# Two groups of values ahead of the recurrence instead of four, and the rest beside its steps

## Chip, cores and metric

The kernel runs on one core of a Trainium2 chip. The metric is the device time of one execution in microseconds (us); lower is better. Engines are called as the profile does: PE (TensorE matmul), PEld (its weight loads), DVE (VectorE), ACT (ScalarE), POOL (GpSimd), SP (SyncE, which issues nearly all DMAs).

## What is computed

A trunk of two layers over 256 tokens of 2048 channels: a pooling mixer and a gated feed-forward block (5632 wide), then an RWKV-7 time mixer and another feed-forward block, and a last norm. The change touches the RWKV-7 mixer alone. Cut to what matters:

```python
xr, xw, xk, xv, xa, xg = (h + xx * mu[j] for j in range(6))   # xx: h shifted by one token, minus h
r, k, v = xr @ w_r, xk @ w_k, xv @ w_v                        # 2048 x 2048 each
w_log, a, g = ...                                             # narrow (LoRA) projections
def step(state, inp):                                         # 32 heads of 64, 256 tokens
    r_t, w_t, k_t, v_t, a_t, b_t = inp
    sa = einsum('bhvk,bhk->bhv', state, a_t)
    state = state * w_t + sa[..., None] * b_t + v_t[..., None] * k_t
    return state, einsum('bhvk,bhk->bhv', state, r_t)
# y: group norm per head, plus a bonus (r k r_k) v, times g, then @ w_o
```

## The kernel before

Matmuls of weights are done in a split form: a weight or an activation is held as a high and a low part of type float32r, and three matmuls (high x high, high x low, low x high) are summed. `split_weights` (L149 to L151) loads a [128, 1024] tile of weights by DMA from SP's queue, makes the high part by a copy on ACT and the low part by a subtraction on DVE. The residual stream `h` is token-major in SBUF.

The recurrence is run in four chunks of 64 tokens, with the heads in 16 pairs, and the pairs in eight groups of two. Per group there are these parts, each written as a Python generator that yields after each *piece*:

- `values(gi)`, 4 pieces: token-major values of a group. A piece is one split tile of weights and 24 matmuls of 128 x 256 (L398 to L400), into one bank of PSUM (`acc`, three banks, shared with the output projection). After the fourth, ACT copies the bank to a tile `vt` (L403). The 16 tiles `xv` that all values read are made by the mix `mu_v`.
- `prepare(gi)`, 7 pieces: decay and rates (L435 to L440), a running sum (L448), decayed keys and receptances KB and AR, which go to DRAM (`dKB`, L474, L475), the triangular matrices M (L485, L487, to `dM`, L489), and the bonus.
- `invert(half)`, 18 pieces, one for each half of the groups: reads M back (L506), does 31 rows of two DVE instructions, each on the result of the one before (L515, L516), stores the result to `dZ` (L519), and a transposed copy (L520) to `dW` (L521). It has no matmul.
- `ready(gi)`, 6 pieces: loads KB and AR back (L714, L715), transposes (L722), makes masked products G of them (L733, L735), loads the inverse's blocks (L745, L748, L750), and joins them with two rounds of small matmuls (L756, L763, copies at L758 and L765).
- `chains(gi)`, 12 pieces: the recurrence proper, three pieces a chunk (L788 and L791; L797, the first that needs the inverse; L802 and L806 with the state's update on DVE).
- `head_norm(gi)` with the gate (L839 to L841), and `out_proj` (L903 to L905), which adds two groups' share of the output projection, 512 columns a piece pair.

`weave(main, others)` issues `main` piece by piece and spreads the pieces of each other generator evenly from a first to a last piece of main. What it writes is an order of priority. A planner (the scheduler of the framework) then goes through all instructions with a timeline of its own: on each engine it takes the first in priority that can run, so later work fills holes; a tile is given when a buffer of its tag is free. The order so found is fixed for each engine's queue.

A group's chains begin `STAG` = 8 steps after those of the group before, so there are 68 steps. Ahead of and beside them, before the change:

- **Stage A**, dense: values of groups 0 to 3 (16 pieces), the gate's narrow projection with its mixes (17 pieces over the first 12), `invert(0)` (18 pieces over the first 14).
- **Stage B**: `LV` = 6 pieces of values of group 4 on; 14 pieces of preparation of groups 4 to 7; `ready(0)`.
- **Stage C**, the 68 steps. Beside them: `ready(1)` to `ready(7)`; the other 10 pieces of values up to step `VL` = 20; the other 14 pieces of preparation up to step `PE_` = 8; `invert(1)` from step 8 to `IE` = 16; normalisation of each group from 12 to 18 steps after its start; the output projection, in parts, from step 26 on.

Preparation of groups 0 to 3 is done earlier, beside the receptances. Values of groups 0 to 3 lie in tiles of the pool `mx`, those of the others in four tiles (`vt`, `bufs=4`) of a pool that opens after stage A. `mx` has `MX` = 40 slots of [128, 512] and holds besides: the mixes `xv`, keys and receptances of the later pairs, KB, AR and their transposes, y, squares, gates, normalised ys, the last projection's weights, and G of groups 4 and 5 (G of groups 0 and 1 lies in `h`, that of others in eight tiles of their own).

Of the kernel before, what the change touches and what calls it, by code (L numbers as in the profile page):

```python
# [29 lines left out]
MX = 40  # L30
# [5 lines left out]
HP, VL, HNL = 30, 20, 6  # L36
LV, LP, PE_, IE = 6, 14, 8, 16
# [7 lines left out]
# columns of the [128, .] table of shape-only constants  # L45
# [3 lines left out]
def _consts():  # L49
    parts = []  # L50

    def put(name, a):
        a = np.ascontiguousarray(a, dtype=np.float32).reshape(128, -1)
        at = sum(p.shape[1] for p in parts)
        _COLS[name] = (at, at + a.shape[1])
        parts.append(a)

    p = np.arange(128)
    put("ident", np.eye(128))
    # pooling over tokens: rows are source tokens of a half, columns target tokens  # L60
    t = np.arange(T)
    p0 = np.zeros((128, 4, 144))
    p1 = np.zeros((128, 4, 128))
    for g, w in enumerate(WINDOWS):
        cnt = np.minimum(t + 1, w)
        band = ((t[None, :] >= t[:, None]) & (t[None, :] < t[:, None] + w)) / cnt[None, :] - np.eye(T)
        p0[:, g] = band[:128, :144]
        p1[:, g] = band[128:, 128:]
    put("pool0", p0)
    put("pool1", p1)  # L70
    # gram masks: rows (k | b) or (b | k), columns (r | a) or (a | r); b carries the factor -1/2
    j = (p % 64)[:, None]
    c = np.arange(64)[None, :]
    incl, strict = (j <= c).astype(np.float32), (j < c).astype(np.float32)
    even_rows = np.where(p < 64, 1.0, -0.5)[:, None]
    odd_rows = np.where(p < 64, -0.5, 1.0)[:, None]
    put("gmask", np.concatenate([incl * even_rows, strict * even_rows, strict * odd_rows, incl * odd_rows], 1))
    put("mmask", strict * -0.5)
    put("scan", np.tile((t % 64 != 0).astype(np.float32)[None], (128, 1)))
    put("twice", p[:, None] % 32 == np.arange(32)[None])  # L80
    put("heads", np.stack([p < 64, p >= 64], 1))
    put("rowscale", np.concatenate([even_rows, odd_rows], 1))
    return np.ascontiguousarray(np.concatenate(parts, 1))
# [7 lines left out]
def hybrid_encoder(ctx: ExitStack, tc: tile.TileContext, I, out):  # L91
# [5 lines left out]
    # residual stream, token-major: h[i][n] is [128 tokens, 512 channels]  # L97
# [28 lines left out]
    def load_sqrt(after):  # L126
        """have the table of Sqrt loaded by the time that its argument is there"""
        nc.scalar.activation(warm, after, AF.Sqrt, bias=epsr[:, 0:1], scale=0.0)
# [3 lines left out]
    # ---------------------------------------------------------------- helpers  # L132
    last = {}       # instructions that others are queued behind
# [4 lines left out]
    def split_weights(src, step=1024, tiles=None):  # L138
        """DRAM [P, n] -> list of (hi, lo) float32r tiles of step columns"""
# [15 lines left out]
    def split_act(dst, src, P=128):  # L155
        """fp32 [P, 256] -> float32r [P, hi 256 | lo 256]"""
        nc.scalar.copy(dst[:P, :256], src)
        nc.vector.tensor_sub(dst[:P, 256:], src, dst[:P, :256].bitcast(F32))
# [17 lines left out]
    def newton(r, v):  # L176
        """one step of r -> r (1.5 - 0.5 v r r); v is overwritten"""
# [4 lines left out]
    # ---------------------------------------------------------------- pooling  # L182
    def pool_layer():
        with tc.tile_pool(name="plc", bufs=1) as pl, tc.tile_pool(name="plp", bufs=1, space=PSUM) as ps:
# [18 lines left out]
            def pooled(g):  # L203
                """weights of a group, its pooled channels"""
# [42 lines left out]
    # ---------------------------------------------------------------- ffn  # L247
    def ffn(layer, each=None):
        gcol = par[f"g2_{layer}"]
        with ExitStack() as st:  # L250
            fg = st.enter_context(tc.tile_pool(name="ffg", bufs=1))     # written last, so in the place of what is read last before
# [62 lines left out]
    # ---------------------------------------------------------------- rwkv  # L314
    def weave(main, *others):
        """issue main piece by piece; others: (generator, its pieces, first and last piece of main to spread them over)"""
# [12 lines left out]
    def chained(*gens):  # L329
        for gen in gens:  # L330
            yield from gen

    def rwkv():
        with ExitStack() as st:
# [12 lines left out]
            # derived per-channel parameters  # L347
# [16 lines left out]
            rn = lp.tile([64, 256], F32R, name="rn")      # per head: hi, and lo below  # L364
            ends = misc[:, 820:884].rearrange("p (a b) -> p a b", b=4)
            bonus = misc[:, 884:948].rearrange("p (a b) -> p a b", b=32)
            kh = (slice(0, 64), slice(64, 128))     # token rows of k in an even and an odd chunk; b has the others

            # scratch: (k | b) and (r | a) of each pair, and the triangular systems of each half of the pairs
# [17 lines left out]
            def values(gi):  # L387
                """token-major values of two head pairs"""
                acc = acc_bank()
                av = acc.rearrange("p (i c) -> p i c", i=2)  # L390
                for u in range(4):
# [9 lines left out]
                    if u == 3:  # L401
                        vts[gi] = mx(F32, "vt") if gi < 4 else late[0].tile([128, 512], F32, name="vt", tag="vt", bufs=4)
                        nc.scalar.copy(vts[gi], acc)  # L403
                    yield

            def placed(tile_, first):
                """[128, 2, 2, 64] view: columns 0:64 of even chunks and 64:128 of odd ones, or the other way"""
# [3 lines left out]
            def narrow(src, P):  # L411
                """DRAM [P, 512] -> its hi and lo"""
# [10 lines left out]
            def prepare(gi, zbank):  # L423
                """two head pairs: decayed keys and rates, their triangular matrices, their bonus; 7 pieces"""
# [3 lines left out]
                for jj in range(2):  # L428
                    # decay and rate: tanh of half the logits
# [13 lines left out]
                for jj in range(2):  # L443
                    j = gi * 2 + jj
                    (thw, tha), k_, r_ = logits[jj], kt[j], rt[j]
                    # log decay, its running sum within a chunk, and the exponentials
# [8 lines left out]
                    # k (1 + (a - 1) k_a), and minus the normalised key  # L455
# [21 lines left out]
                    # M[j, t] per head and chunk, on the rows of b  # L477
# [12 lines left out]
                    # bonus: sum over the head of r k r_k  # L490
# [7 lines left out]
            def invert(half):  # L498
                """(I - M)^-1 of the 32x32 diagonal blocks of eight pairs: one system per partition; 18 pieces"""
# [10 lines left out]
                for t in range(31, 0, -1):  # L510
                    # rows above t take their share of row t
# [12 lines left out]
            # ---- projections that see all channels; the residual stream waits in DRAM meanwhile  # L524
            kt, rt, xv, vts, late = [], [], [], {}, []
            with tc.tile_pool(name="rp1", bufs=1) as p1:
# [24 lines left out]
                def mix_tile(name, k):  # L551
                    """h + (shifted(h) - h) mu, split"""
# [11 lines left out]
                def project(src, xs, dst):  # L564
                    """one tile of 128 output channels; 2 pieces"""
# [12 lines left out]
                def loras(srcs, names, m, fns, dsts):  # L578
                    """two narrow projections side by side in a bank, the mixes made on the way; 17 pieces"""
# [31 lines left out]
                def project_first():  # L611
                    """the first tiles side by side, while the mixes are still being made; 6 pieces"""
# [13 lines left out]
                def head_norms(j):  # L626
                    """the squares of a tile's keys, added up by head"""
# [39 lines left out]
                for k in range(16):  # L667
# [8 lines left out]
                weave(chained(values(0), values(1), values(2), values(3)),  # L676
                      (loras(I["ga"], ("mu_g", "mu_g"), 128, (AF.Sigmoid, AF.Sigmoid), hid[2:]), 17, 0, 12),
                      (invert(0), 18, 0, 14))
# [23 lines left out]
            def ready(gi):  # L702
                """what the chains of two pairs need: masked products of (k | b) with (r | a), (k | b) token-major,
                and the inverses of the 64x64 systems joined from those of their halves; 6 pieces"""
                half, at = gi // 4, (gi % 4) * 8
                z = Z[gi % 3]
                w11 = pt = c2.tile([128, 8, 32], F32, name="w11", tag="w11", bufs=1)       # rows of the upper and of the lower blocks
                m12 = c2.tile([128, 8, 32], F32, name="m12", tag="m12", bufs=1)
                AR[gi], KBT[gi], G[gi] = [], [], []
                for jj in range(2):  # L710
# [7 lines left out]
                    # (k | b) token-major  # L718
# [49 lines left out]
            def chains(gi):  # L768
                """two head pairs, chunk after chunk; 12 pieces"""
# [3 lines left out]
                # v in the token rows of k, what the recurrence adds in those of b: even chunks in the one tile, odd ones in the other  # L773
# [47 lines left out]
            def all_chains():  # L821
                """the chains of a group begin before those of the group before end"""
# [7 lines left out]
            def gating(gi):  # L830
                """the gate of two head pairs, channel-major"""
# [13 lines left out]
            def head_norm(gi, i0=0, i1=2):  # L845
                """group norm over a head, bonus, gate of some halves of the tokens; channel-major and split; 4 pieces"""
# [46 lines left out]
            def out_proj(pairs):  # L893
                """the share of some pairs of heads in the output projection; a piece for each two pairs and 512 columns"""
# [16 lines left out]
            def last_weights():  # L911
                """the output projection's weights for the last two pairs; 4 pieces"""
# [11 lines left out]
            def last_proj(i):  # L924
                """the share of the last two pairs, for half of the tokens; 4 pieces"""
# [15 lines left out]
            vals = chained(*(values(g) for g in range(4, 8)))  # L941
# [8 lines left out]
            # pieces of the values, of the preparation and of the output projection that fill in beside the chains  # L950
            assert IE <= 3 * STAG and PE_ <= IE
            weave(itertools.islice(vals, LV), (itertools.islice(prep, LP), LP, 0, LV), (ready(0), 6, 1, LV))
            more = [(ready(g), 6, STAG * g - STAG, STAG * g - RE) for g in range(1, 8)]
            more += [(head_norm(g), 4, STAG * g + 12, STAG * g + 12 + HNL) for g in range(7)]
            more += [(vals, 16 - LV, 0, VL), (prep, 28 - LP, 0, PE_), (invert(1), 18, PE_, IE), (reload(), 1, STAG + 12, STAG + 13)]
# [17 lines left out]
    # ---------------------------------------------------------------- all  # L973
# [28 lines left out]
def _layout(inp):  # L1002
# [14 lines left out]
    def side_by_side(*tiles):  # L1017
        """[L, 128, 16 x 128] each; 4 tiles of the one, 4 of the other, and so on"""
# [33 lines left out]
```

## Time and profile before

| | |
|---|---|
| time, three runs | 2220.01 us (median), 2218.32, 2232.19 |
| span of the profiled execution | 2233.6 us (no other time is given for it) |
| PE busy, PEld, DVE, ACT | 98%, 85%, 62%, 49% of the span |
| mean granted clock of PE | 0.970 |
| moved by DMA | 395.10 MB |

The span counts from the first to the last instruction. A matmul's recorded duration reaches over the start of the next one, so PE's throughput is read from starts, not from durations. `PEclk` is the share of PE's full clock that the throttle granted. Line numbers are those of the kernel before; stage A begins at about 1030 us and the layer ends at about 1482 us.

### The profile page before, as it was taken

The numbers are of one execution on the slowest core, as the hardware profiler recorded it, in microseconds if no ns is written. First come the engines' busy times: TensorE is split into PE (matmuls) and PEld (weight loads), VectorE is DVE, ScalarE is ACT, GpSimd is POOL, SyncE is SP. The second block draws the span as 40 slices with busy tenths as digits, with TensorE's granted clock in tenths as the row PEclk, the third lists the DMA queues.
The fourth block names the chain that finished last, engine by engine and source line by source line (L and its number), as shares of the span: only waits on it lengthen the run. The fifth ranks groups of instructions, "written<-read, shape, count | busy, mean of one in ns | idle before, by whom it ended". The sixth has DMA issues, their size and how long they took to land.

```text
span 2233.6 us, 34461 instructions
## 1 busy us (share of the span) xinstructions
PE 2180.7 (98%) x13402; PEld 1891.7 (85%) x13402; DVE 1383.9 (62%) x2190; ACT 1100.6 (49%) x1824; POOL 28.6 (1%) x72
## 2 busy tenths in 40 slices
PE   7999999999999989999999999999999999999997
PEld 5888888888888889999998888778888888888886
DVE  8666666666444488678766466766666666654444
ACT  5544444445434478665544244544444444444443
POOL 0000000000000000011000000000000000000000
PEclk9999999999999999999996599999999999999999
DMA  6555555555555544566654143425555555555554
GB/s 230 170 188 189 188 188 186 187 187 187 202 196 205 204 143 168 181 205 195 205 164 136 56 130 109 157 91 189 188 189 188 188 189 188 188 192 193 193 193 151
DMA packets 147044, 395.10 MB, mean 177 GB/s; under 512 B 39232, under 2 KB 46784, under 8 KB 146496
## 3 DMA queue, kind: packets, MB, share of 16 engines
q1 hardware_dynamic: 145728, 390.80, 53.1%
q8 instruction: 105, 1.72, 0.3%
q10 hardware_dynamic: 1152, 2.10, 0.3%
q14 instruction: 59, 0.48, 0.1%
HBM read 376.59 MB, written 16.25 MB: 176 GB/s over the span
## 4 chain that ended last, share of the span: by engine, by line
PE 91%; DVE 4%; DMA 2%; ACT 1%; issue 1%; SPq 0%; ACTq 0%; DVEq 0%
PE acc L280 29%; PE acc L281 15%; PE acc L305 7%; PE acc L306 7%; PE acc L307 7%; PE acc L573 2%; PE acc L571 2%; PE acc L572 2%; DVE wl L151 2%; PE cb L788 2%; PE g L733 1%; PE acc L904 1%; PE acc L903 1%; PE acc L905 1%; PE acc L399 1%; PE acc L398 1%
## 5 line engine op out<-in xcount | busy, mean ns | idle before, releaser
L151 DVE TENSOR_TENSOR wl<-raw,wh 128x1024 fp32r<-128x1024 f32 x661 | 807.5, 1222 | 623.2 <-ACT wh L150 610.8
L150 ACT CAST wh<-raw 128x1024 fp32r<-128x1024 f32 x661 | 691.9, 1047 | 752.0 <-PE acc L307 267.7
L280 PE MATMUL acc<-xs,wh 128*128 128x512 f32 x2816 | 965.5, 396 | 4.9 <-DVE xs L264 4.4
L281 PE MATMUL acc<-xs,wl 128*128 128x256 f32 x2816 | 731.5, 280 | 0.1
L280 PEld LDWEIGHTS acc<-xs,wh 128*128 128x128 f32 x2816 | 504.3, 188 | 100.1 <-DVE xs L264 6.1
L281 PEld LDWEIGHTS acc<-xs,wl 128*128 128x128 f32 x2816 | 529.1, 188 | 33.6 <-DVE wl L151 2.0
L306 PE MATMUL acc<-wl,gT 128*128 128x512 f32 x704 | 274.3, 390 | 2.0 <-DVE wl L151 2.0
L307 PE MATMUL acc<-wh,gT 128*128 128x512 f32 x704 | 273.9, 389 | 0.0
L305 PE MATMUL acc<-wh,gT 128*128 128x512 f32 x704 | 245.5, 389 | 0.1
L306 PEld LDWEIGHTS acc<-wl,gT 128*128 128x128 f32 x704 | 132.2, 188 | 30.6 <-DVE wl L151 3.3
L305 PEld LDWEIGHTS acc<-wh,gT 128*128 128x128 f32 x704 | 131.9, 188 | 27.9 <-ACT wh L150 0.5
L307 PEld LDWEIGHTS acc<-wh,gT 128*128 128x128 f32 x704 | 132.2, 188 | 27.5
L573 PE MATMUL acc<-mx,wl 128*128 128x256 f32 x464 | 133.1, 287 | 3.7 <-DVE wl L151 3.7
L571 PE MATMUL acc<-mx,wh 128*128 128x256 f32 x464 | 132.2, 285 | 0.0
L572 PE MATMUL acc<-mx,wh 128*128 128x256 f32 x464 | 131.9, 284 | 0.0
L283 ACT COPY t<-acc 128x256 f32<-128x256 f32 x88 | 32.8, 372 | 130.6 <-PE acc L281 130.6
L573 PEld LDWEIGHTS acc<-mx,wl 128*128 128x128 f32 x464 | 88.6, 191 | 5.5 <-DVE wl L151 5.3
L571 PEld LDWEIGHTS acc<-mx,wh 128*128 128x128 f32 x464 | 88.6, 191 | 0.8
L572 PEld LDWEIGHTS acc<-mx,wh 128*128 128x128 f32 x464 | 88.7, 191 | 0.0
L399 PE MATMUL acc<-wl,mx 128*128 128x256 f32 x256 | 75.4, 295 | 1.2 <-DVE wl L151 1.1
L398 PE MATMUL acc<-wh,mx 128*128 128x256 f32 x256 | 74.1, 290 | 0.0
L400 PE MATMUL acc<-wh,mx 128*128 128x256 f32 x256 | 74.0, 289 | 0.0
(287 smaller groups left out, 2334.6 us busy)
## 6 DMA issues: line engine op xcount, KB each, us to landing
raw<-in_w SPq DMA_DIRECT2D x528, 512.0 KB, 4.4
raw<-in_wk SPq DMA_DIRECT2D x32, 512.0 KB, 4.0
raw<-in_wr SPq DMA_DIRECT2D x32, 512.0 KB, 4.4
raw<-in_wv SPq DMA_DIRECT2D x32, 512.0 KB, 4.2
raw<-in_wo SPq DMA_DIRECT2D x32, 512.0 KB, 4.0
raw<-in_pw SPq DMA_DIRECT2D x8, 512.0 KB, 7.1
dKB<-KB SPq DMA_DIRECT2D x16, 256.0 KB, 2.3
dKB<-AR SPq DMA_DIRECT2D x16, 256.0 KB, 2.6
```

The source lines that it names most:

```text
L150: nc.scalar.copy(wh[:P, :step], raw[:P, :step])
L151: nc.vector.tensor_sub(wl[:P, :step], raw[:P, :step], wh[:P, :step].bitcast(F32))
L280: nc.tensor.matmul(acc, lhsT=w[:, cs], rhs=xs[k], start=(k == 0), stop=False, skip_group_check=True)
L281: nc.tensor.matmul(acc[:, :256], lhsT=l[:, cs], rhs=xs[k][:, :256], start=False, stop=(k == 15), skip_group_check=True)
L305: nc.tensor.matmul(acc[i], lhsT=gh, rhs=w[:, cs], start=(k == 0), stop=False)
L306: nc.tensor.matmul(acc[i], lhsT=gh, rhs=l[:, cs], start=False, stop=False)
L307: nc.tensor.matmul(acc[i], lhsT=gl, rhs=w[:, cs], start=False, stop=(k == FT - 1))
L398: nc.tensor.matmul(av[:, i], lhsT=xh, rhs=w[:, cs], start=(k == 0 and i == 0), stop=False, skip_group_check=True)
L399: nc.tensor.matmul(av[:, i], lhsT=xh, rhs=l[:, cs], start=False, stop=False, skip_group_check=True)
L571: nc.tensor.matmul(acc[:, :256], lhsT=w[:, cs], rhs=xs[k][:, :256], start=(k == 0), stop=False)
L572: nc.tensor.matmul(acc[:, :256], lhsT=w[:, cs], rhs=xs[k][:, 256:], start=False, stop=False)
L573: nc.tensor.matmul(acc[:, :256], lhsT=l[:, cs], rhs=xs[k][:, :256], start=False, stop=(k == 15))
```

## The change

Numbers and three places in the weaving change:

```diff
-MX = 40
+MX = 44
-HP, VL, HNL = 30, 20, 6
-LV, LP, PE_, IE = 6, 14, 8, 16
+HP, VL, HNL = 30, 46, 6
+VF = 2
+LV, LP, PE_, IE = 4, 0, 12, 20
...
-  vts[gi] = mx(F32, "vt") if gi < 4 else late[0].tile([128, 512], F32, name="vt", tag="vt", bufs=4)
+  vts[gi] = mx(F32, "vt") if gi < VF else late[0].tile([128, 512], F32, name="vt", tag="vt", bufs=4)
...
-  weave(chained(values(0), values(1), values(2), values(3)),
-        (loras(I["ga"], ("mu_g", "mu_g"), 128, (AF.Sigmoid, AF.Sigmoid), hid[2:]), 17, 0, 12),
-        (invert(0), 18, 0, 14))
+  weave(chained(*(values(g) for g in range(VF))),
+        (loras(I["ga"], ("mu_g", "mu_g"), 128, (AF.Sigmoid, AF.Sigmoid), hid[2:]), 17, 0, 4 * VF),
+        (invert(0), 18, 0, 4 * VF))
...
-vals = chained(*(values(g) for g in range(4, 8)))
+vals = chained(*(values(g) for g in range(VF, 8)))
 prep = chained(*(prepare(g, g_bank) for g in range(4, 8)))
...
-weave(itertools.islice(vals, LV), (itertools.islice(prep, LP), LP, 0, LV), (ready(0), 6, 1, LV))
+weave(itertools.islice(vals, LV), (itertools.islice(prep, LP), LP, 0, LV), (ready(0), 6, 0, LV))
 more = [(ready(g), 6, STAG * g - STAG, STAG * g - RE) for g in range(1, 8)]
 ...
-more += [(vals, 16 - LV, 0, VL), (prep, 28 - LP, 0, PE_), (invert(1), 18, PE_, IE), ...]
+more += [(vals, 4 * (8 - VF) - LV, 0, VL), (prep, 28 - LP, 0, PE_), (invert(1), 18, PE_, IE), ...]
```

So stage A has values of groups 0 and 1 only, with the gate's projection and `invert(0)` spread over their eight pieces; stage B has the four pieces of group 2 and `ready(0)`, and no preparation; stage C has 20 pieces of values up to step 46, all 28 pieces of the late preparation up to step 12, and `invert(1)` from step 12 to 20. Values of groups 2 to 7 share the four tiles `vt`. The amount of computation is the same. (The diff also drops comments.)

More of the change, by code (lines that the diff above doesn't have):

```diff
@@ L948, in reload @@
                 yield
-            assert IE <= 3 * STAG and PE_ <= IE
-            weave(itertools.islice(vals, LV), (itertools.islice(prep, LP), LP, 0, LV), (ready(0), 6, 1, LV))
+            assert IE <= 3 * STAG and PE_ <= IE and VL <= 6 * STAG
+            weave(itertools.islice(vals, LV), (itertools.islice(prep, LP), LP, 0, LV), (ready(0), 6, 0, LV))
             more = [(ready(g), 6, STAG * g - STAG, STAG * g - RE) for g in range(1, 8)]
             more += [(head_norm(g), 4, STAG * g + 12, STAG * g + 12 + HNL) for g in range(7)]
-            more += [(vals, 16 - LV, 0, VL), (prep, 28 - LP, 0, PE_), (invert(1), 18, PE_, IE), (reload(), 1, STAG + 12, STAG + 13)]
+            more += [(vals, 4 * (8 - VF) - LV, 0, VL), (prep, 28 - LP, 0, PE_), (invert(1), 18, PE_, IE), (reload(), 1, STAG + 12, STAG + 13)]
             for first, count in OB_:
```

## The prediction

> **What bounds the kernel now.** The page comes first: TensorE is the engine that is never free, and the slices with the clock show one place where it is slow.
>
> ```profile
> PE 2180.7 (98%) x13402; PEld 1891.7 (85%) x13402; DVE 1383.9 (62%) x2190; ACT 1100.6 (49%) x1824; POOL 28.6 (1%) x72
> ...
> PEclk9999999999999999999996599999999999999999
> ```
>
> One slice is 55.8 us, so the two low slices lie around 1190 to 1290 us. Next I cut the stretch from the first values to the end of the layer into windows at the events that matter (columns: busy time and count of PE, its weight loads, DVE, ACT and POOL, then granted clock, DMA share, GB/s).
>
> ```profile
> 1030.00:1085.00 55.00, 54.08 (x445) 53.47 (x446) 50.96 (x116) 34.76 (x66) 2.26 (x3) 1.00 0.49 164
> 1085.00:1146.40 61.40, 59.18 (x520) 54.38 (x519) 33.95 (x63) 30.91 (x58) 3.46 (x12) 0.92 0.66 208
> 1146.40:1191.20 44.80, 44.38 (x481) 39.52 (x480) 32.77 (x70) 26.08 (x60) 3.51 (x9) 1.00 0.49 155
> 1191.20:1290.20 99.00, 97.14 (x587) 80.64 (x587) 53.57 (x145) 31.90 (x75) 3.55 (x6) 0.52 0.31 89
> 1290.20:1440.00 149.80, 148.51 (x1264) 119.21 (x1264) 102.77 (x205) 71.41 (x155) 0.61 (x1) 0.97 0.39 122
> 1440.00:1482.00 42.00, 39.38 (x198) 31.47 (x196) 32.16 (x65) 15.22 (x30) 0.00 (x0) 0.95 0.38 136
> ```
>
> Two readings. The first window is bound twice: PE is busy 98% and DVE 93% (50.96 of 55). The fourth has PE busy for 97 of 99 us at a granted clock of 0.52: it is busy because it is slow. The timeline shows what the clock does to one kind of matmul, first at the low clock, then at the full one:
>
> ```profile
> 1121.89 0.41 PE L398 MATMUL acc<-wh,mx 128*128 128x256 f32 x1
> 1122.10 0.41 PE L399 MATMUL acc<-wl,mx 128*128 128x256 f32 x1
> ...
> 1123.44 0.28 PE L400 MATMUL acc<-wh,mx 128*128 128x256 f32 x1
> 1123.56 0.28 PE L398 MATMUL acc<-wh,mx 128*128 128x256 f32 x1
> ```
>
> Start to start, 0.21 us against 0.12 us. So the fourth window costs up to 99.0 x (1 - 0.52) = **47.5 us** more than the same matmuls would at full clock. Why is it low there? What ran when it was high:
>
> ```profile
> L398 PE MATMUL acc<-wh,mx x256: 278/283/415, 1029.5 to 1184.9; 128*128 128x256 f32 x128
> L905 PE MATMUL acc<-wh,ys x112: 387/393/793, 1234.5 to 1469.6; 128*128 128x512 f32 x112
> L797 PE MATMUL cb<-rhs,Z x256: 218/218/367, 1146.4 to 1453.6; 64*64 64x64 f32 x128
> ```
>
> The values' dense matmuls (L398 to L400) end at 1185, the clock is down from 1191; the output projection (L905 stands for it) begins at 1234 and its bulk comes later. Between them PE has the recurrence's small blocks (L797: 64x64) and what prepares them. I read the low clock as a lack of dense filler, which the traces can test.
>
> **The change part by part.**
>
> *Values leave the first window (eight pieces).* A group of values is 4 pieces of 24 matmuls, so two groups are 192 x 0.12 = 23.0 us of PE. But DVE works here on the first inverse and on the gate's mixes, and these stay. What leaves DVE is eight splits of weights; their cost stands in the windows of that line alone:
>
> ```profile
> 1030.00:1085.00 55.00, 17.53 (x15) 1.00 0.49 164
> L515 DVE TENSOR_TENSOR sysP<-sysM,sysZ x62: 191/357/426, 1024.3 to 1280.3; 128x31 f32<-128x31 f32 x4, 128x60 f32<-128x60 f32 x4, 128x87 f32<-128x87 f32 x4, 128x112 f32<-128x112 f32 x4
> L520 ACT COPY sysM<-sysZ x2: 2016/2076/2135, 1084.4 to 1285.9; 64x1024 f32<-64x1024 f32 x2
> ```
>
> 17.53 / 15 = 1.17 us, eight are 9.4 us; at the 93% that DVE reaches now, 10.1 us. The first inverse, whose last act is the copy at L520, ends at 1084.4 - 10.1 = 1074.3 (bounds 0, if splits of the third group move into the hole, to 23). ACT (34.76 of 55) does not bind. So 13 of the 23 us that leave PE are not saved; PE waits there for DVE.
>
> *From the inverse to the first step that needs it.* The first L797 starts at 1146.4, 62.0 us after L520. That path is one copy, the triangular systems out and in by DMA through SP's queue, two small matmul rounds with copies:
>
> ```profile
> L521 SPq DMA_DIRECT2D dW<-sysM x2: 461/484/508, 1086.6 to 1288.0; - x2
> ...
> DMA to landing us min/median/max: 2.9/4.2/5.6
> ...
> L745 SPq DMA_DIRECT2D Z<-dZ x32: 303/448/871, 1091.6 to 1358.6; - x32
> ...
> DMA to landing us min/median/max: 1.6/2.4/7.0
> L758 ACT COPY w<-g x16: 363/364/367, 1134.0 to 1395.8; 32x256 f32<-32x256 f32 x16
> ```
>
> Copy 2.1, out 4.2, eleven issues of loads at 0.45 on SP 5.0, landing 2.4 to 7.0, four copies of 0.36 and two rounds of matmuls with their hand-overs about 4: **18 to 23 us** if nothing is in the way. Today the stretch is filled: the row of the values' L399 in the second window (below) counts 93 of them, 93 x 3 x 0.12 = 33.5 us of PE, beside two of the last four groups of preparation (eight L435 there, four a group). After the change four pieces of values (11.5 us) and no preparation are due ahead of it. I take 30 us, between the bare path and the present one and nearer the bare one: first L797 at 1104, **-42 us** (bounds 20 and 47 us for the path).
>
> *What the recurrence must take in.* Counts of L399 by window:
>
> ```profile
> L399 PE MATMUL acc<-wl,mx x93: 274/283/415, 1084.8 to 1145.9; 128*128 128x256 f32 x93
> L399 PE MATMUL acc<-wl,mx x47: 278/283/387, 1149.6 to 1185.1; 128*128 128x256 f32 x47
> L435 PE MATMUL g<-hid,lbh x8: 283/349/580, 1086.1 to 1118.7; 96*128 96x256 f32 x8
> L435 PE MATMUL g<-hid,lbh x8: 280/283/384, 1146.8 to 1174.8; 96*128 96x256 f32 x8
> L149 SPq DMA_DIRECT2D raw<-in_wv x32: 327/332/1182, 1015.4 to 1158.1; - x32
> ```
>
> 47 x 3 = 141 values matmuls lie after 1146.4 today; five groups make 480. The 339 more cost 339 x 0.12 = 40.7 us of PE. Two more groups of preparation come in: 12 matmuls at 0.12 each (L435 to L437) and some thirty small ones, 3.5 us a group by 7 in the third window's rate; 7 us. Together **+48 us** of PE. DVE: 14 more splits x 1.17 = 16.4, and the two groups of preparation cost less than all that DVE did in the third window, where two groups ran (32.77). At most 49 us, and the low-clock window has 99.0 - 53.57 = 45.4 free. DVE is about covered, not comfortably; should it not be, the excess is 4 us and more cold clock. Fourteen loads of values move on SP's queue past the recurrence's own, 14 x 0.33 = 4.7 us in some 150 us, and POOL, with 3.55 of 99 us, takes the preparation's few small copies; both at nothing, since the wide window moves bytes for 0.31 of it only. The copy of a finished group of values now waits on ACT for one of four tiles; behind it stand copies of the recurrence, but ACT has 67 of 99 us free, so I price it at nothing too, up to a few us a group.
>
> *The cold stretch.* At the third window's rate, 47 L399 in 44.8 us, the 160 L399 of five groups last 152 us: from 1104 to about 1256, where the output projection, due from step 26 of 68, takes over. So the filler bridges the hole: **-47.5 us** at best. But the second inverse (steps 12 to 20) brings no matmul, and the written spread of values, 20 pieces over 46 steps, is thin: 0.43 x 2.9 = 1.25 us of dense work a step. I leave a quarter of the stretch cold: **+12 us** (bounds 0 and 47.5).
>
> *Slots.* Forty slots become 44, while the sixteen tiles that feed the values (xv) are now held until the last values are made. I price the wait at nothing in the sum; it is the second rival.
>
> **Sum.** -42 + 48 - 47.5 + 12 = -29.5, so about **30 us less**. The page's span is 2233.6; the three times shown are 2218.3, 2220.0 and 2232.2, and nothing beside the span is given for the profiled execution. It lies 13.6 over the median. I apply the difference to the median: **2190 us**. If the 13.6 us were part of the cold stretch, the gain on the median would be 16 us and the time 2204.
>
> The Trainium skill, "TensorE: Matmul & The Clock Gate", Part 1, says that the clock comes back after one busy window of some 3.4 us and drops after an idle one. The row that bears on it disagrees in part: PE was 98% busy for 99 us at 0.52, so busy alone did not bring it back here. The same page's caveats say that the gate has been seen stuck low for over 50 us; by that the stretch would have no cause in the work and could return, which is what the first rival prices by rows.
>
> **Rivals.**
>
> *The clock stays down although there is filler.* Recurrence steps break up the dense work, and the stretch returns whole: -42 + 48 = +6, that is 2226; with half of it, 2202. For it: PE was packed in the cold stretch, and output projection matmuls from 1229 on did not lift it before 1259. Against it: the third window, with the same recurrence steps and values between them, ran 44.8 us at 1.00.
>
> *The slots run out (the slower case).* Count about steps 32 to 40: xv 16, AR and KBT of three groups 10 to 12, two loads, four groups of masked products in this pool 8, y 3, ys 6 to 8, gates and squares 3: some 50 for 44. It decides if values are still to be made when groups 4 and 5 are made ready; their last two cannot end early, since six groups share four tiles for values (vt), and the fifth of these waits for the normalisation of group 2 at step 34. Then loads of (k | b) wait for slots, as one does now in the chain that ended last:
>
> ```profile
> 1107.20 4.12 DMA KB<-dKB
> ```
>
> Ten such waits (two pairs in five groups) of 4.1 us are 41 us, and PE idle for that long loses its clock (it did here: low from 1112.7). 2190 + 41 = 2231, and with all 35 us of the cold stretch back 2266; since the waits bring some of it back, 2240 to 2266, and I take 2250.
>
> *The planner does not follow the spread.* Weaving sets priorities; today ten pieces spread over 20 steps were done by 1185, about step 11. If it fills every hole so, no cold quarter remains and the path after the inverse is the bare one: -42 - 7 + 48 - 47.5 = -48, 2172.
>
> A page speaks for the slots too: the Trainium skill, "Perfetto Trace Analysis", Identifying Performance Opportunities, says that a gap that repeats can mean too little SBUF for the next tile. No run here shows it yet.
>
> **How the numbers follow.** Forecast (2175 to 2208): 0.53. Planner fills all (2155 to 2175): 0.12. Clock stays down, half to whole (2202 to 2230): 0.18. Slots (2240 to 2266): 0.17. The range leaves out most of the slots' case and the best end: **2160 to 2236**. A measurement of this kernel tells about 1% (22 us) from no change; below 2198 is faster. Of the forecast 0.8 lies there: 0.43, with 0.12 is 0.55, and a little of the clock's case, 0.57. Slower (over 2242): 0.15. The rest, 0.28, is the same.
>
> **What would show it.** Last L520-type copy of the first inverse at about 1074; first L797 near 1104; values' last matmul beyond 1230 rather than at 1185; granted clock over 0.85 in the hundred us before the output projection. Wrong would be: first L797 after 1125 (the sum's first term), a clock of about 0.5 for over 60 us (the third), or waits on KB loads at every group (slots).

## Result and profile after

The changed kernel takes **2251.46 us** (median of four runs, 2246.82 to 2258.55; the kernel before beside it 2219.16). The ratio is 1.0111, with an interval of 1.007 to 1.0153: slower by about 25 us (32 by these two medians) where 30 us less were forecast. The profiled execution took 2252.45 us, 1.75 of them outside its span of 2250.7. From L397 on, line numbers after are those of before plus one. In this section "after" is the changed kernel.

The page of after: busy time, and the granted clock in 40 slices.

```profile
PE 2188.8 (97%) x13402; PEld 1899.5 (84%) x13402; DVE 1384.0 (61%) x2190; ACT 1103.0 (49%) x1824; POOL 27.8 (1%) x72
...
PEclk9999999999999999999985899899999999999999
```

The low clock has not gone: four slices, within a stretch of six, lie below 0.9 where before had two. Next after's windows (columns as in the prediction): stage A, then the stretch from the first step that needs the inverse.

```profile
1030.00:1085.00 55.00, 54.03 (x439) 52.62 (x439) 51.56 (x114) 34.32 (x70) 1.88 (x2) 1.00 0.57 190
...
1109.20:1173.60 64.40, 60.11 (x549) 54.22 (x548) 36.81 (x82) 31.89 (x74) 3.76 (x15) 0.84 0.45 144
1173.60:1235.00 61.40, 53.73 (x362) 46.78 (x360) 42.91 (x112) 23.27 (x58) 4.21 (x10) 0.53 0.45 138
```

Stage A is as packed as it was (DVE 51.56 of 55, before 50.96). The hundred us before the output projection hold a window at 0.53 in which PE, moreover, is free for 7.7 us. Three views of single lines of after say when things happened: the inverse's copy, the first matmul that needs the inverse, and one of the three lines of the values, asked by stretch.

```profile
L521 ACT COPY sysM<-sysZ x2: 2095/2108/2120, 1092.8 to 1278.0; 64x1024 f32<-64x1024 f32 x2
...
L798 PE MATMUL cb<-rhs,Z x256: 218/218/366, 1109.2 to 1470.9; 64*64 64x64 f32 x128
...
L399 PE MATMUL acc<-wh,mx x93: 279/283/385, 1033.6 to 1084.2; 128*128 128x256 f32 x93
L399 PE MATMUL acc<-wh,mx x44: 274/283/386, 1085.5 to 1108.4; 128*128 128x256 f32 x44
L399 PE MATMUL acc<-wh,mx x55: 274/283/561, 1111.0 to 1165.1; 128*128 128x256 f32 x55
L399 PE MATMUL acc<-wh,mx x1: 415/415/415, 1233.8 to 1233.8; 128*128 128x256 f32 x1
L399 PE MATMUL acc<-wh,mx x63: 276/283/583, 1244.4 to 1367.0; 128*128 128x256 f32 x63
```

The recurrence starts 37.2 us earlier (1109.2 against 1146.4). Values of groups 2 to 5 are done by 1165; then one matmul of this line in 79 us; then groups 6 and 7 (63 of the 119 such matmuls that come after the first step) between 1244 and 1367, in the midst of the output projection, which begins at 1232. The planner did not carry the filler into the hole. What stood in the way shows in the copies that make the high parts of the weights (L151), of which these are the first three after 1166; the tile `wh` that they write has two buffers (`WB` = 2).

```profile
1173.29 1.04 ACT L151 CAST wh<-raw 128x1024 fp32r<-128x1024 f32 x1 [0.76 <-DMA raw<-in_wo]
1175.72 1.03 ACT L151 CAST wh<-raw 128x1024 fp32r<-128x1024 f32 x1
...
1245.55 1.05 ACT L151 CAST wh<-raw 128x1024 fp32r<-128x1024 f32 x1
```

The first is a tile of the output projection, which PE uses from 1231.9 on. The second is the first piece of group 6: its load was issued at 1169.2 and its low part was done at 1178.6, but PE's order has its first matmul at 1233.8 and the rest from 1244 on. So both buffers were held for some 55 us, and no further values could be split meanwhile. Why the planner chose this order is not shown.

To see where the 37 us went, both kernels are cut at the same steps of the recurrence (first matmul that needs the inverse, then each quarter of these matmuls, the last one, and the start of the feed-forward block). Before:

```profile
1146.40:1237.40 91.00, 89.17 (x756) 77.19 (x755) 61.83 (x148) 40.48 (x96) 5.22 (x12) 0.75 0.44 130
1237.40:1329.60 92.20, 91.75 (x614) 74.23 (x613) 49.21 (x111) 34.04 (x72) 1.83 (x3) 0.71 0.34 102
1329.60:1389.90 60.30, 60.30 (x578) 49.23 (x577) 40.76 (x82) 29.65 (x67) 0.61 (x1) 1.00 0.38 116
1389.90:1458.30 68.40, 67.11 (x493) 53.52 (x493) 52.62 (x109) 32.95 (x68) 0.00 (x0) 0.95 0.42 145
1458.30:1482.90 24.60, 21.08 (x91) 16.67 (x88) 17.37 (x36) 8.39 (x19) 0.00 (x0) 0.93 0.19 64
```

After:

```profile
1109.20:1221.30 112.10, 100.14 (x840) 89.37 (x839) 67.84 (x162) 51.60 (x122) 7.37 (x24) 0.71 0.46 140
1221.30:1308.30 87.00, 86.44 (x698) 73.49 (x697) 60.69 (x142) 36.60 (x77) 2.07 (x3) 0.82 0.39 117
1308.30:1400.20 91.90, 91.90 (x704) 74.47 (x703) 49.64 (x91) 36.72 (x74) 0.61 (x1) 0.94 0.39 123
1400.20:1473.50 73.30, 72.30 (x502) 56.97 (x501) 49.50 (x99) 33.14 (x65) 0.00 (x0) 0.88 0.38 128
1473.50:1500.40 26.90, 23.75 (x111) 19.10 (x108) 22.37 (x50) 12.65 (x29) 0.00 (x0) 1.00 0.29 83
```

The first quarter takes 21 us longer, at a lower clock and with PE free for 12.0 us where it was free for 1.8; the third takes 31.6 us longer with PE never free (91.90 of 91.90) and 126 more matmuls.

**What low clock costs.** The mean granted clock is known for every timed run of the experiments. The same kernel, before, ran 102 times beside them, on three chips, with clocks from 0.969 to 0.986, and its span followed:

| clock of the run (before) | runs | mean span, us |
|---|---|---|
| 0.970 | 4 | 2235.3 |
| 0.973 | 11 | 2229.4 |
| 0.976 | 14 | 2223.7 |
| 0.980 | 5 | 2216.6 |
| 0.983 | 4 | 2210.4 |

A line through all 102 has a slope of 18.1 us for each 0.01 of clock (correlation -0.97); the means are 2224.4 us and 0.9757, and on each chip the mean span lies within 0.5 us of that. A microsecond at half clock takes 0.5 us off clock x span, so by this line it costs 0.41 us. The last columns of the table below set each kernel's mean span against that line: so much the clock explains, so much is left. A correlation alone does not say that the clock drives the time; e10 tests that. Three executions far off all others (one each of e5, e8 and e11: 4591.72, 5892.64 and 2650.77 us) are left out of the mean spans.

### The profile page after: what moved, and what is told of

Same layout as the page of the kernel before. It is cut to its first block, busy times and chain, and to the rows that moved or that the text cites. A ratio compares the mean times of both kernels' runs of the same rounds, so it can differ in the third digit from the quotient of the medians.

```text
span 2250.7 us, 34472 instructions
## 1 busy us (share of the span) xinstructions
PE 2188.8 (97%) x13402; PEld 1899.5 (84%) x13402; DVE 1384.0 (61%) x2190; ACT 1103.0 (49%) x1824; POOL 27.8 (1%) x72
## 5 line engine op out<-in xcount | busy, mean ns | idle before, releaser
L151 ACT CAST wh<-raw 128x1024 fp32r<-128x1024 f32 x661 | 692.3, 1047 | 748.4 <-PE acc L308 267.2
L399 PE MATMUL acc<-wh,mx 128*128 128x256 f32 x256 | 77.6, 303 | 0.0
L401 PE MATMUL acc<-wh,mx 128*128 128x256 f32 x256 | 76.8, 300 | 0.0
```

The source lines that it names most:

```text
L151: nc.scalar.copy(wh[:P, :step], raw[:P, :step])
L399: nc.tensor.matmul(av[:, i], lhsT=xh, rhs=w[:, cs], start=(k == 0 and i == 0), stop=False, skip_group_check=True)
```

## Experiments

Times are medians; the ratio is to runs of the kernel before taken beside them. "d" is mean span less 2224.4.

| run | us | ratio, interval | clock | d | by clock | left |
|---|---|---|---|---|---|---|
| after | 2251.46 | 1.0111 [1.007, 1.0153] | 0.9685 | +25.9 | +13.0 | +12.8 |
| e1 values by step 26 | 2225.48 | 0.9991 [0.9963, 1.0019] | 0.9771 | -2.8 | -2.6 | -0.2 |
| e2 preparation and inverse alone | 2255.93 | 1.0131 [1.0077, 1.0185] | 0.9662 | +28.9 | +17.1 | +11.8 |
| e3 before, long dense | 2237.52 | 1.0048 [1.0025, 1.0071] | 0.9882 | +9.9 | -22.7 | +32.6 |
| e4 after, long dense | 2271.56 | 1.0211 [1.0165, 1.0257] | 0.9775 | +46.7 | -3.3 | +50.0 |
| e5 preparation alone | 2227.05 | 1.0005 [0.9971, 1.0039] | 0.9737 | -0.1 | +3.7 | -3.7 |
| e6 inverse alone | 2244.98 | 1.0103 [1.0025, 1.0181] | 0.9697 | +18.3 | +10.8 | +7.6 |
| e7 spread of values alone | 2239.05 | 1.0055 [1.003, 1.008] | 0.9694 | +12.8 | +11.4 | +1.4 |
| e8 e1, inverse as before | 2229.23 | 1.0007 [0.9977, 1.0038] | 0.9727 | +1.2 | +5.5 | -4.3 |
| e9 after, inverse as before | 2262.52 | 1.0154 [1.0119, 1.019] | 0.9652 | +34.1 | +19.1 | +15.0 |
| e10 before, short dense | 2213.86 | 0.9953 [0.9926, 0.9979] | 0.9839 | -9.7 | -14.9 | +5.2 |
| e11 e1, short dense | 2220.05 | 0.997 [0.9946, 0.9994] | 0.9828 | -6.5 | -12.9 | +6.4 |
| e12 after, short dense | 2241.76 | 1.0085 [1.0058, 1.0112] | 0.9777 | +15.8 | -3.7 | +19.5 |
| e13 after, thin late values | 2233.9 | 1.0026 [0.9998, 1.0055] | 0.9684 | +7.1 | +13.2 | -6.1 |
| e14 e1, thin values | 2229.81 | 1.0019 [0.9991, 1.0047] | 0.9685 | +3.7 | +13.0 | -9.3 |
| e15 before, more short dense | 2219.55 | 0.9972 [0.9946, 0.9998] | 0.9878 | -6.5 | -22.0 | +15.6 |

The theories: **A**, values that come late, beside the output projection, cost; **B**, the preparation (B1) or the later second inverse (B2) beside the steps costs; **C**, time follows the granted clock, and dense matmuls lift it; **D** denies C.

### Which part of the change costs

**e1**, the change with the values due sooner.

```diff
-HP, VL, HNL = 30, 46, 6
+HP, VL, HNL = 30, 26, 6
```

> The changed kernel with VL = 26 instead of 46: all values are due before step 26, where the output projection begins, so that the planner puts the values of groups 6 and 7 ahead of it. Theory A (a hole: from 1171 to 1244 us PE has no dense filler, since the values of groups 6 and 7 stand behind the first output projection in PE's order; the clock falls to 0.53 there, and later the two kinds of filler get in each other's way): the last values matmul starts before 1240 instead of at 1367, and the time falls by 15 to 35, to 2216 to 2236. Theory B (load: the preparation and the second inverse, moved beside the steps, keep DVE and ACT busy and lengthen the steps, whatever the filler): within 10 of 2251.

One number takes the 25 us back; A's result. The same cuts as above, for e1:

```profile
1108.60:1217.20 108.60, 101.53 (x1010) 91.91 (x1009) 75.01 (x165) 58.75 (x128) 12.29 (x24) 0.93 0.55 174
1217.20:1303.20 86.00, 84.10 (x603) 69.97 (x602) 56.71 (x140) 32.97 (x74) 2.60 (x3) 0.69 0.32 94
1303.20:1377.20 74.00, 74.00 (x618) 59.48 (x617) 46.42 (x89) 33.78 (x71) 1.06 (x1) 0.95 0.40 127
1377.20:1440.00 62.80, 61.85 (x475) 49.23 (x474) 45.68 (x93) 31.64 (x64) 0.00 (x0) 0.97 0.40 133
```

In the first quarter e1 does 170 matmuls more than after in 3.5 us less: its clock there is 0.93, not 0.71. It then reaches the half only 5 us ahead (1303.2 against 1308.3) but with all values done, and the second half has nothing but steps and output projection: 136.8 us against 165.2.

**e2**, the settings of before with the preparation beside the steps and the second inverse due later.

```diff
-LV, LP, PE_, IE = 6, 14, 8, 16
+LV, LP, PE_, IE = 6, 0, 12, 20
```

> One part alone: four groups of values precede the recurrence as before (VF = 4, LV = 6, VL = 20), but all late preparation and the second inverse are beside the steps as in the changed kernel (LP = 0, PE_ = 12, IE = 20). Theory A: the values end where they ended before, so the time is that of before within 12, 2207 to 2231. Theory B: most of the loss is here, 2235 to 2255.

Slower by 29 us, 0.9 over B's range and far from A's. The inverse's second copy in e2 (the last start in the row), and from the waits of 1280 to 1340 us what PE then waits for (us in total, times, longest):

```profile
L521 ACT COPY sysM<-sysZ x2: 1945/2016/2088, 1084.7 to 1322.5; 64x1024 f32<-64x1024 f32 x2
```

```profile
PE g L757 <- DMA w<-dW: 5.5, 1, 5.5
```

It comes at 1322.5; before had it at 1285.9, after at 1278.0. So e2's loss is not simply a part of after's. **e5** and **e6** take it apart.

```diff
-LV, LP, PE_, IE = 6, 14, 8, 16
+LV, LP, PE_, IE = 6, 0, 8, 16      # e5
+LV, LP, PE_, IE = 6, 14, 12, 20    # e6
```

> The settings of before (four groups of values ahead, the other four due by step 20, the second inverse due by steps 8 to 16), with one move alone: the late preparation of readying groups 2 and 3 goes out of the fourteen late pieces ahead and stands beside the steps. It differs from e2 in the inverse's due steps alone (8 to 16 here, 12 to 20 there). Theory B1 (the moved preparation is what costs, by its splits and scans on VectorE between the steps): the loss of e2 comes again, 2243 to 2262 us, first L798-type use near 1123, inverse's second copy still after 1300. Theory B2 (it is the later due steps of the second inverse: nothing waits for it in time): the loss goes, 2212 to 2234 us, with the second copy near 1285 as in before. Theory A (only values beside the output projection cost): 2212 to 2232 us here too, and e2's loss is left without a cause.

> The settings of before with the due steps of the second inverse and its preparation moved from 8 and 16 to 12 and 20, nothing else. Theory B2: slower, 2238 to 2258 us, second copy after 1310. Theory B1: as before, 2214 to 2234 us. Theory A: as before, 2214 to 2232 us.

The moved preparation is free, and the later inverse costs 18 us in e6, with a wide interval (four runs) and 11 of the 18 going with the clock: both times lie in B2's ranges. Details of the expectations failed: in e6 the second copy came at 1289, not after 1310, so it is not lateness at the joining alone; in e5 it came at 1259, not near 1285; and e5's first step came at 1130.0, 16 us before that of before, without a gain at the end.

**e7**, the spread of values alone; **e8** and **e9**, the change with the inverse due as before, with and without the late values.

```diff
 # e7, on before
-HP, VL, HNL = 30, 20, 6
+HP, VL, HNL = 30, 46, 6
 # e8 and e9, on after; e8 has VL = 26 besides
-LV, LP, PE_, IE = 4, 0, 12, 20
+LV, LP, PE_, IE = 4, 0, 8, 16
```

> The settings of before with the values of the four groups behind spread to step 46 instead of step 20, nothing else. Theory A (values that come after the output projection has begun cost, about 25 us for the two groups in after): here also two or three groups come behind the start of the output projection, so slower by 15 to 35, 2235 to 2258 us, last values matmul after 1340. Theory B (values cost nothing where they stand, the loss is the preparation's or the inverse's): 2214 to 2232 us. If the early values were the gain of e1 and not the late ones its loss, also 2214 to 2232.

> The changed kernel with the values due by step 26 instead of 46 (as e1) and the second inverse due by steps 8 and 16 as in before. Theory B2 (the later inverse costs): better than e1 and than before, 2190 to 2215 us. Theory B1 (the moved preparation itself costs): as e1, 2215 to 2235 us. Theory A: as e1, 2215 to 2232 us, since the late values are gone already.

> The changed kernel with one setting taken back: the second inverse and its preparation due by steps 8 and 16 as in before; values still due by step 46. After stands 25 us over before. The runs so far, set against their mean granted clock (runs of before: 1 us of span for each 0.00053 of clock), leave after, e2 and e6, which all have the later inverse, about 12, 11 and 7 us that the clock doesn't explain, and e1, e5, e7, e8 between -4 and +1. Theory B2 (the later inverse costs about 12, the late values cost through the clock alone, about 13): 2233 to 2243 us. Theory A (in the change as a whole the values of groups 6 and 7 beside the output projection cost all of it, the inverse nothing): 2244 to 2258 us. If the inverse were all of it: 2218 to 2230 us.

e7 is slower by 13 us, near the low end of A's range; 11 of the 13 are clock. One group of values (32 matmuls of L399, from 1229 to 1349), not two or three, comes there behind the start of the output projection. e8 is no better than e1 and e9 no better than after but 8 us worse, above every theory's range: so B2 falls for the change as a whole. From e1 to after the late values cost 29 us, from e8 to e9 33. Why the later inverse costs in e2 and e6 and not here stays open; I only see that it goes with values due by step 20.

### Whether the clock is a cause

**e3** and **e4** add 36 dense fp32 matmuls, whose results are thrown away, to the readying of groups 2 and 3, in before and in after.

```diff
+def dense(bank_, gi, x):
+    for _ in range(3 if gi in (2, 3) else 0):
+        nc.tensor.matmul(bank_.rearrange("p (c t) -> p c t", c=4), lhsT=x[:, 0], rhs=x, start=True, stop=True, skip_group_check=True)
...
 p_ = g_bank()
+dense(p_, gi, kb)      # ahead of the transposes
...
 p_ = g_bank()
+dense(p_, gi, ar)      # ahead of each masked product
```

> The kernel before, with work added whose results are overwritten: each of the 12 banks that making ready groups 2 and 3 fills (steps 8 to 24) first gets three dense float32 matmuls of 128 x 128 by 512; 36 in all, about 0.87 us each at full clock by the rows of 128 x 128 float32 blocks (0.11 us for each of two passes), so 31 us more PE work. If the low clock is what the stretch from 1191 to 1290 costs and dense work lifts it (theory A): the time at low clock falls from about 119 us by half or more and the time is between 2195 and 2222 in spite of the added work. If the clock is not the price, or does not rise (theory B): 2235 to 2250.

> The same 36 dense matmuls in the changed kernel. Theory A: they fall into its hole (1171 to 1244), the clock stays higher there and the time is 2225 to 2252, no more than the changed kernel's 2251. Theory B: 2262 to 2282.

Their rows in e3 (each matmul leaves two records; busy us, mean ns), from the groups by line and form, and the clock from its page:

```profile
L705 PE MATMUL g<-AR 128*128 128x512 f32 x48 | 22.6, 603 | 0.0
L705 PE MATMUL g<-KB 128*128 128x512 f32 x24 | 12.3, 651 | 0.6 <-DMA KB<-dKB 0.6
```

```profile
PEclk9999999999999999999999999999999999999999
```

The clock is at 0.9 or more in every slice. Both times lie in B's ranges all the same. The added work explains that: in e3 it costs 35 us by these rows, which less 22.7 us by the clock is +12, and +9.9 was measured. In e4 the rest grows by 37.2 us over after and the clock gives 16.3 back. I first read e3 as a proof that low clock is cheap on this path; the table of the 102 runs shows that this was wrong.

**e10**, **e11**, **e12** and **e15** therefore add 36 short ones (one pass over the finished tiles `hid`), in before, in e1, in after; e15 has 72, in groups 2 to 5.

```diff
+def dense(bank_, gi):
+    for _ in range(3 if gi in (2, 3) else 0):      # e15: (2, 3, 4, 5)
+        nc.tensor.matmul(bank_, lhsT=hid[3][:, :128], rhs=hid[2], start=True, stop=True, skip_group_check=True)
```

> Before with the same 36 extra matmuls at the same places as e3 (readying of groups 2 and 3; their results are thrown away), but one-pass ones on finished tiles, about 9 us of TensorE work in place of 31 to 35. Theory C (the time follows the granted clock at the price that the runs of before show, and filled TensorE time lifts it): clock near 0.983 in place of 0.976, so -13 by the clock and +9 by the work, 2214 to 2226 us; if the short ones lift it as far as e3's 0.988, 2208 to 2216. Theory D (only long dense work lifts it, or low clock is worth little on this path): 2226 to 2240 us with the clock where before has it.

> e1 (the changed kernel with the values due by step 26) with e10's 36 short matmuls. Theory C: clock 0.984 or more, 2210 to 2222 us, under before. Theory D: 2226 to 2240 us.

> The changed kernel with e10's 36 short dense matmuls in the readying of groups 2 and 3. Theory C (half of after's loss is the lower granted clock, 0.9685 against 0.9757): the clock rises by about 0.008 as in e10, -15 by the clock, +5 for the work, 2236 to 2246 us. If the clock of after is only a mark of waits and not their cause: clock and time as after, 2250 to 2260 us.

> Before with 72 short dense matmuls, in the readying of groups 2 to 5 instead of 2 and 3 (e10). Work +10 us (e10's 36 cost about 5). Theory C with clock left to win (e10 still had 65 us of low clock, 48 of them after 1200 us): clock near 0.989, -24 + 10, 2208 to 2214 us. If e10 has won what there is: 2216 to 2224 us.

C in e10, e11 and e12, with small misses (e10 is 0.1 us under C's first range, e11's clock 0.9828 instead of 0.984), and D in none of them; e15 is mixed. e10's added line, by its instructions, and then its four quarters, cut at the same steps as before:

```profile
L705 PE MATMUL g<-hid x36: 387/496/795, 1190.5 to 1236.8; 128*128 128x512 f32 x36
```

```profile
1143.50:1239.80 96.30, 94.44 (x794) 79.67 (x793) 61.65 (x148) 41.06 (x96) 5.23 (x12) 0.84 0.41 124
1239.80:1318.40 78.60, 78.57 (x600) 63.71 (x600) 49.57 (x112) 32.72 (x70) 1.78 (x3) 0.80 0.39 115
1318.40:1381.70 63.30, 63.30 (x591) 51.82 (x590) 41.27 (x84) 30.68 (x67) 0.61 (x1) 1.00 0.39 121
1381.70:1437.30 55.60, 53.66 (x444) 42.26 (x444) 42.87 (x92) 29.71 (x62) 0.00 (x0) 1.00 0.39 123
```

Work that computes nothing makes before **faster**, by 0.2 to 0.7%: 14.9 us by the clock for 5.2 us of work. It is the fastest version of this study, ahead of both kernels. The same in after gives 10 us of the lost 25 (e12), with the clock up by 0.009. Twice as many (e15) lift the clock again, but the rest grows by 10 us for 7 us by the clock; e15's time stood at the middle of the second case it was given, that e10 had won what there is. The same in e1 (e11) wins 4 us of span where e10 wins 10; the clock rises by 0.006 instead of 0.008.

### What the same values cost early and late

**e13** (on after) and **e14** (on e1) leave out two of the three products in the values of groups 6 and 7: 128 matmuls, 15.4 us at 0.12. Loads and splits stay, and the planner orders the rest anew; these two groups' values are those of the high halves alone.

```diff
 nc.tensor.matmul(av[:, i], lhsT=xh, rhs=w[:, cs], ...)
+if gi >= 6:
+    continue
 nc.tensor.matmul(av[:, i], lhsT=xh, rhs=l[:, cs], ...)
 nc.tensor.matmul(av[:, i], lhsT=xl, rhs=w[:, cs], ...)
```

> The changed kernel with two of the three products of each block left out in the values of groups 6 and 7 (so their values are those of the high halves alone); loads, splits, copies and order stay. 128 matmuls of 0.12 us at full clock, 15 us. Theory P (late values cost as TensorE work, where TensorE is never free): 2228 to 2238 us. Theory Q (they cost by their splits on VectorE, their loads or their place in the order, the matmuls are hidden): 2244 to 2256 us.

> e1 (values due by step 26) with the same 128 matmuls left out of groups 6 and 7. If the early place charges them at full price as the late one would: 2204 to 2212 us, 14 to 18 under e1's 2225. If they are worth something there as dense filler (the clock of e1's first quarter, 0.93, falls toward after's 0.71): 2216 to 2232 us, with the mean clock under 0.975.

Late, the 128 matmuls cost 17.6 us, at an unchanged clock: theory P. Early, leaving them out saves nothing (4.3 us more by the medians, 6.5 by the means): the clock falls from 0.9771 to 0.9685, worth 15.6 us, as much as the work at 0.12. e14's first quarter, beside e1's above, shows it:

```profile
1108.20:1221.30 113.10, 102.31 (x881) 90.94 (x880) 74.73 (x167) 58.16 (x128) 8.83 (x24) 0.73 0.52 165
```

129 matmuls fewer, 4.5 us more, clock 0.73 instead of 0.93. So the change's loss has a size that can be put together from runs: 192 matmuls of two groups, at 17.6 us for 128, would be 26.4 us late and nothing early; after stands 28.6 us of span over e1.

The Trainium skill, "TensorE: Matmul & The Clock Gate", Terms, prices low clock as the time spent low times (1 - K/N), half of it here. By the 102 runs it is 0.41 instead of 0.5, so the rule comes out about a fifth too high for this kernel, whose PE is 98% busy.

## Why the prediction was wrong

**The step that failed is the cold stretch**, -47.5 and +12 of the sum. Its price was somewhat high (0.5 us for each us at half clock, measured 0.41, so about 39 us for that window and not 47.5), and its cause was right (dense filler lifts the clock: e10, e12, e14). What failed is that the filler would be there. "160 L399 of five groups last 152 us" took the rate of one window for the rate of all; in fact groups 2 to 5 were used up by 1165 and the planner put groups 6 and 7 behind the start of the output projection. Time at low clock in the profiled executions, from 1000 us on, was 122.9 us after and 119.5 before; the runs' means give +13 us where -35.5 was put down.

**Intake, +48, was counted at one place.** The spread work was taken to be the same wherever it lies. For 128 of its matmuls e13 and e14 show full price late and nothing early. By count it was smaller than forecast, too: 119 matmuls of L399 lie after the first step (55 + 1 + 63), 47 did before, so 72 x 3 x 0.12 = 25.9 us instead of 40.7: stage A ran 93 of them where two groups have 64, and the stretch from there to the first step 44 and not 32.

**First inverse at 1074.3: wrong, by its own bound.** It came at 1092.8. The sentence had the bound "0, if splits of the third group move into the hole"; L399 x93 in 55 us is nearly three groups of values, so they did. The copy came 8.4 us after even that bound; 4.1 us of this were there before the stage began (first L399 at 1033.6, L398 of before at 1029.5), and the rest is not explained. **The path of 30 us** then took 16.4, under the 18 to 23 that I called bare. The two errors cancel, which is luck: -37.2 for -42.

**DVE about covered: held.** DVE was busy for 42.91 of 61.40 us in the window from 1173.6 on; e5 prices the moved preparation at -0.1 us in all, where the sum had +7 for its work on PE. For the inverse, whose later steps were given no price at all, e6 has 18 us, but e9 against after has -8.

**PE's free time was left out of the sum.** From first step to feed-forward PE is free for 16.7 us after and 7.1 before (the five rows of each). In the profiled pair this closes most of the account, with the prediction's +7 for the preparation left in: -37.2, +25.9, +7, +9.6 free, +7.9 of clock (each row's length times one less its clock: 62.5 us lost over after's rows, 54.6 over before's) are +13.2; the feed-forward block starts 17.5 us later. Some 4 us stay unexplained.

**The 13.6 us over the median** go with the clock, as the prediction allowed for: the profiled run of before had 0.970, and such runs take 2235.3 us.

**The rivals.** "The clock stays down although there is filler" is nearest to what happened, with the mechanism the other way round: the clock stayed down because there was none. Its price of +6 was too low: it had neither the free time (+9.6 above) nor more low clock than before (+7.9). The slots gave 2250 and so, by luck, the right number for a reason that did not occur: the waits on loads of (k | b) in all of after are these (us in total, times, longest),

```profile
PE g L723 <- DMA KB<-dKB: 5.0, 3, 3.9
```

5 us and not 41 (and of the load of 4.1 us that this rival counted ten times, PE was idle for 1.98 us in before); the program built with 40 or 48 slots in place of 44 has the same order of instructions on every engine. "The planner does not follow the spread" was right on that point and wrong on its sign: it served groups 2 to 5 at once and left the last two for the worst place.

The signs it named: copy at 1092.8 for 1074 (wrong), first step at 1109.2 for 1104 (right), last values beyond 1230 (1367, right, and just that was the harm), clock over 0.85 ahead of the output projection (0.53 in the last 61 us, wrong).

## What to carry to other kernels

Filler for a stretch that lacks dense matmuls must be shown to lie *in* that stretch: read the planned order, and ask of every moved piece whether TensorE is free, low-clocked, or full where it lands; the same 128 matmuls cost 17.6 us in one place and nothing some 135 us earlier. Where runs of one kernel differ by a per cent, set their times against their granted clock before comparing kernels, and split a loss into what the clock explains and what is left. If the clock is low in a stretch of small blocks, a few dense matmuls, useful ones or not, can be worth more than they cost (36 of them: -10 us here).

## What was not expected of the hardware

- One program, 102 runs, one core of each of three chips: granted clock 0.969 to 0.986, span 2205 to 2238 us, correlation -0.97. The same instruction stream does not get the same clock each time.
- TensorE was busy for 97 of 99 us at a clock of 0.52 in before, with the recurrence's small blocks and, from 1230 on, 30 matmuls of 128 x 512. 36 more of these within 46 us (e10) raised the mean clock of the runs from 0.9757 to 0.9839; the time at low clock went from 119.5 to 64.9 us in the profiled executions, of which that of before was one of the slower.
- Taking 15 us of matmuls out of e1 made it no faster (2229.81 against 2225.48 us), as the clock fell by 0.0086.
